# A hybrid decoder layer on one core: other first loads, memory work behind the queries, and another order of the last dense products

## The chip, the core and the metric

The kernel runs on one core of one Trainium2 chip. Every time is in device microseconds (us); a run's time is that of the whole program on that core, and a comparison uses medians of several runs. The profile is one execution with the hardware profiler on. Engines are called as in the profile: PE (TensorE), DVE (VectorE), ACT (ScalarE), POOL (GpSimd), SP (SyncE, which here only issues loads).

## What is computed

One layer for 256 tokens of 1024 channels, with 256 memory tokens. Three branches read the same normalised input: a diagonal state-space layer with a gated unit behind it, a sparse attention (an indexer picks 64 keys for each query), and a cross-attention into the memory. Each is projected up, gated and summed, then projected out; a mixture of 32 experts follows.

```python
h = rms_norm(x, g_mix)
u_ssm, q, k, v, qi, ki, wi, qm, gates = split(h @ w_in)
km, vm = split(rms_norm(mem, g_mem) @ w_mem_kv)
y_ssm = s5_branch(u_ssm, ...)      # ends in y * sigmoid(y @ w_glu)
y_dsa = dsa_branch(q, k, v, qi, ki, wi, positions)
y_mem = memory_branch(qm, km, vm)
g_s, g_d, g_m = split(sigmoid(gates))
merged = g_s * (y_ssm @ w_up_ssm) + g_d * (y_dsa @ w_up_dsa) + g_m * (y_mem @ w_up_mem)
x = x + merged @ w_out
x = x + hier_moe(rms_norm(x, g_ffn), ...)   # 32 experts, 2 chosen for a token
```

## The kernel before

**Dense part.** Every product with a weight of the first part is a `job`, cut into quarters of two 128-row blocks. There are 70 quarters, numbered here 0 to 69 in the order in which the jobs are created: u 0 to 3, a (indexer, keys, values) 4 to 7, q 8 to 11, km, qm and vm (memory keys, queries, values) 12 to 23, the gates 24 to 47, and then the up-projections m 48 to 51 and d 52 to 55, the gated unit glu 56 and 57, the up-projection s 58 to 61, and the output projection o 62 to 69. A quarter's weights (512 KB) are loaded four quarters ahead (`load_quarter`) into the buffers RAW and are split into a high and a low part: ACT copies the high part (L241), DVE subtracts for the low one (L242), into three rotating buffers SPL. `product` then runs twelve matmuls on PE (L257 to L259). In the loop over the quarters, `split(q + 2)` stands ahead of `product(q)`.

**What runs in between.** Three generators, a (attention), s (state space) and m (memory), are advanced one step at a time after each half quarter, as the string table STEPS says. `finish(...)` runs the rest of a generator where its result is needed. The steps use PE for small matmuls, ACT, DVE and POOL. In the attention a `scores` step is PE L739, DVE L815 (mask and maximum), ACT L708 (exponentials), DVE L710 and L712 and POOL L712 (division); a `values` step is PE L718 (transposes), ACT L719, PE L827, then ACT L724 and DVE L725 (`y_split`). The memory's values are PE L883. The state-space layer hands its result to glu through ACT L685 and DVE L686, which write the operand `ysp`; behind glu stand PE L534 (transposes), DVE L693, ACT L695 and DVE L696. `merged_T` transposes the merged branches for the output projection.

**Experts.** 192 pieces of 1 MB of expert weights, two to a matrix, are loaded in order into a ring (RING) of 11 units of two slots each. The slots are those of the dense part; `feed` issues the next piece when its slot is free (`there`), in the dense part by the conditions at the end of the quarter loop, in the expert part when a slot has been read (`release`). A unit that is an entry of GEN2 is one buffer, whose halves come free only together. The experts' products (L1267 gate and up, L1319 down) follow a short router stage.

Instructions go to each engine's queue in an order that a scheduler sets from the program order and priorities; `manual_schedule` keeps program order on the engine named. An engine runs its queue in order.

## Time and profile before

| | |
|---|---|
| time, median of 3 runs | 732.78 us (731.33 to 732.97) |
| time of the profiled execution | 733.47 us |
| its span, first to last instruction | 731.7 us |
| busy in the span: PE, DVE, ACT, POOL | 79%, 42%, 29%, 11% |
| granted PE clock, mean | 0.926 |
| moved by DMA | 246.78 MB |

1.8 us of the profiled execution lie outside its span. The shares are averages over a dense part (to about 280 us) and an expert part with quite different limits, so the rows further down go by stretches.

### The profile page before, as it was taken

To read this page: it belongs to the slowest core of one execution; us is meant where nothing else is said; L and a number is where in the kernel's file an instruction comes from. 1 tells how busy PE (TensorE), PEld (TensorE's weight loads), DVE (VectorE), ACT (ScalarE), POOL (GpSimd) and SP (SyncE) were. 2 spreads that over 40 slices of the span, in tenths; PEclk is the share of its full clock that TensorE was granted. 3 is DMA by queue.
4 is the path that set the end of the run, shared out by engine and by line. 5 is a ranking of instruction groups with operands and counts; after the bars stand their busy time and mean duration, and the time that the engine had idled before them with its cause. 6 is when DMAs were issued, how large, how long until landed. Compare 5 with 4: busy or idle time off the path is not lost.

```text
span 731.7 us, 12785 instructions
## 1 busy us (share of the span) xinstructions
PE 581.6 (79%) x5284; PEld 374.3 (51%) x5284; DVE 308.0 (42%) x772; ACT 211.5 (29%) x426; POOL 77.5 (11%) x122
## 2 busy tenths in 40 slices
PE   8889999999998999888676685495577668469765
PEld 4677787786876786444343252252233324234423
DVE  5999999999574755222120021021111012001102
ACT  6776764648743452111100001000000000000002
POOL 2722201001022001202020020001002002000000
PEclk9999999999999999999996799789879789789989
DMA  8874334436757979999999999999999999999992
GB/s 313 317 217 143 125 118 135 144 118 227 276 175 286 320 299 402 428 425 419 431 424 422 430 428 422 428 427 421 429 426 425 427 426 421 429 426 425 420 409 105
DMA packets 31358, 246.78 MB, mean 337 GB/s; under 512 B 3904, under 2 KB 4544, under 8 KB 15936
## 3 DMA queue, kind: packets, MB, share of 16 engines
q1 hardware_dynamic: 30352, 244.87, 83.4%
q8 instruction: 43, 0.70, 0.4%
q0 software_dynamic: 512, 0.53, 0.3%
q10 hardware_dynamic: 432, 0.52, 0.2%
q14 instruction: 19, 0.16, 0.1%
HBM read 244.33 MB, written 1.05 MB: 335 GB/s over the span
## 4 chain that ended last, share of the span: by engine, by line


## 5 line engine op out<-in xcount | busy, mean ns | idle before, releaser
L1267 PE MATMUL w<-arena 128*32 128x256 f32 x1088 | 125.1, 456 | 43.0 <-DMA arena<-w_up 31.0
L1267 PE MATMUL w<-s,arena 128*32 128x256 f32 x960 | 111.8, 439 | 30.7 <-DMA s<-w_up 29.6
L258 PE MATMUL pj<-s,s 128*128 128x512 f32 (+1 forms) x280 | 112.5, 402 | 4.8 <-DVE s L242 4.8
L257 PE MATMUL pj<-s,s 128*128 128x512 f32 (+1 forms) x280 | 110.0, 405 | 7.0 <-ACT s L241 3.4
L259 PE MATMUL pj<-s,s 128*128 128x512 f32 (+1 forms) x280 | 110.3, 397 | 0.1
L1267 PEld LDWEIGHTS w<-arena 128*32 128x32 f32 x1088 | 55.5, 130 | 90.0 <-DMA arena<-w_up 37.1
L242 DVE TENSOR_TENSOR s<-arena,s 128x1024 fp32r<-128x1024 f32 (+2 forms) x71 | 87.0, 1230 | 21.5 <-ACT s L241 20.9
L241 ACT CAST s<-arena 128x1024 fp32r<-128x1024 f32 (+2 forms) x71 | 72.7, 1029 | 47.3 <-PE pj L259 27.6
L1267 PEld LDWEIGHTS w<-s,arena 128*32 128x32 f32 x960 | 50.5, 125 | 69.0 <-DMA s<-w_up 35.8
L1225 POOL TENSOR_SCALAR s<-early,s 128x32 f32<-128x32 f32 x64 | 32.3, 522 | 350.0 <-PE w L1231 295.6
L1324 DVE COPY arena<-w 32x256 f32<-32x256 f32 x62 | 25.9, 418 | 91.4 <-PE w L1319 78.2
L1324 ACT COPY arena<-w 32x256 f32<-32x256 f32 x62 | 22.5, 364 | 143.7 <-DVE arena L1324 143.7
L257 PEld LDWEIGHTS pj<-s,s 128*128 128x128 f32 x280 | 52.4, 189 | 21.8 <-ACT s L241 6.7
L258 PEld LDWEIGHTS pj<-s,s 128*128 128x128 f32 x280 | 53.1, 190 | 18.8 <-DVE s L242 8.5
L1305 DVE TENSOR_TENSOR early<-w,early 64x256 f32<-64x256 f32 x16 | 6.8, 428 | 126.9 <-ACT early L1304 126.9
L259 PEld LDWEIGHTS pj<-s,s 128*128 128x128 f32 x280 | 53.0, 190 | 10.5 <-DVE s L696 0.5
L1304 ACT ACTIVATE misc<-w 64x256 f32<-64x256 f32 x16 | 6.0, 375 | 137.0 <-PE w L1267 137.0
L1319 PE MATMUL w<-s,s 128*32 128x256 f32 x544 | 34.8, 397 | 10.4 <-DVE s L1310 6.1
L1319 PE MATMUL w<-arena,s 128*32 128x256 f32 x448 | 32.2, 434 | 9.5 <-DMA arena<-w_down 6.0
L1304 ACT ACTIVATE early<-w 64x256 f32<-64x256 f32 x16 | 6.0, 377 | 115.6 <-PE w L1267 115.6
L1305 DVE TENSOR_TENSOR misc<-w,misc 64x256 f32<-64x256 f32 x16 | 6.8, 426 | 72.6 <-ACT misc L1304 72.6
L1260 DVE TENSOR_TENSOR arena<-w,misc 128x256 f32<-128x256 f32 x32 | 12.1, 420 | 57.1 <-PE w L1257 57.1
(307 smaller groups left out, 690.0 us busy)
## 6 DMA issues: line engine op xcount, KB each, us to landing
arena<-w_up SPq DMA_DIRECT2D x15, 2048.0 KB, 29.5
arena<-w_gate SPq DMA_DIRECT2D x13, 2048.0 KB, 29.5
arena<-w_down SPq DMA_DIRECT2D x12, 2048.0 KB, 30.7
s<-w_down SPq DMA_DIRECT2D x12, 2048.0 KB, 31.9
s<-w_gate SPq DMA_DIRECT2D x11, 2048.0 KB, 34.3
s<-w_up SPq DMA_DIRECT2D x9, 2048.0 KB, 34.2
s<-w_up SPq DMA_DIRECT2D x13, 1024.0 KB, 27.1
arena<-w_g SPq DMA_DIRECT2D x24, 512.0 KB, 3.9
```

Of the source, the lines that this page charges most:

```text
L241: S.copy(hi[:, c], src[:, c])
L242: V.tensor_tensor(lo[:, c], src[:, c], hi[:, c], ALU.subtract)
L257: PE.matmul(ps, lhsT=lh, rhs=hi[:, k], start=kt == 0, stop=False)
L258: PE.matmul(ps, lhsT=lh, rhs=lo[:, k], start=False, stop=False)
L259: PE.matmul(ps, lhsT=ll, rhs=hi[:, k], start=False, stop=kt == j["kts"] - 1)
L1225: G.tensor_scalar(dst[:, tt, :], iota[:, 0:CAP], col[:, tt:tt + 1], fac[:, tt:tt + 1], ALU.is_equal, ALU.mult)
L1260: V.tensor_tensor(xe[:, h], xg[:, k:k + 2], b_(gff[:, h], 128), ALU.mult)
L1267: PE.matmul(gu[32 * q:32 * q + 32, :], lhsT=xe[:, kt, 32 * j:32 * j + 32], rhs=w[:, kt % 4, 256 * (q % 2):256 * (q % 2) + 256], start=kt = ...
L1304: S.activation(sg[64:128, :], gu[0:64, :], AF.Silu)
L1305: V.tensor_tensor(hid, gu[64:128, :], sg[64:128, :], ALU.mult)
L1319: PE.matmul(dn[32 * q:32 * q + 32, :], lhsT=hd[:, kb, 32 * c:32 * c + 32], rhs=w[:, kb, 256 * q:256 * q + 256], start=c + kb == 0, stop=c ...
L1324: (S.copy if q % 2 else V.tensor_copy)(Y[32 * j:32 * j + 32, 256 * q:256 * q + 256], dn[32 * q:32 * q + 32, :])
```

## The change

First loads: the first two blocks of the transposed input and g8 are issued from ACT's queue, the weights of quarter 0 from SP's at once; SP keeps program order up to quarter 11 and again from quarter 40. The second half of `x` and `early` are issued behind the first weights of a. The memory tokens are loaded at quarters 8 and 11 rather than 6, qm is computed ahead of km, and the generator m splits its input before it sums its squares.

Last dense products: the order becomes glu (48, 49), m (50 to 53), s (54 to 57), d (58 to 61), then o. `finish(m)` stands at quarter 46, `finish(s)` at 48, `finish(a)` at 58. STEPS spreads the attention's steps out to quarter 60.

Ring: units are taken in another order, by when their slots come free, and `share` paces the pieces during the dense part to 0.75 MB-pieces a quarter with at most two in hand, until the last six quarters.

```diff
-STEPS = ("||s|s|s||sa|a|saa||s|ss|s|s|mm|mm|samm|amm|samm|amm|sa|a|sa|a|sa|a|sa|a|sa|a|sa|a|sam|am|sam|a|sa|a|"
+STEPS = ("|||||s|s|s||sa|a|saa||s|ss|s|sa|sa|sa|a|sam|am|sam|am|samm|am|samm|am|sam|am|sa|a|sam|am|sam|a|sa|a|"
...
-    SP.dma_start(g8, A["g8"])
-    SP.dma_start(xT_raw[:, 0:2], A["xT"][:, 0:2])
+    first = ExitStack()
+    first.enter_context(tc.manual_schedule(engines={mybir.EngineType.SP}))
+
+    S.dma_start(xT_raw[:, 0:2], A["xT"][:, 0:2])
+    S.dma_start(g8, A["g8"])
+    S.dma_start(xT_raw[:, 2:4], A["xT"][:, 2:4])
...
-            for c in ((slice(0, w), slice(w, 2 * w)) if q == 0 else (slice(0, 2 * w),)):
+            for c in ((slice(0, w), slice(w, 2 * w)) if q < 2 else (slice(0, 2 * w),)):
...
-                (V if n == "s" else G).tensor_tensor(m, m, gt, ALU.add)
+                (V if n == "d" else G).tensor_tensor(m, m, gt, ALU.add)
...
-    for n in ('km', 'qm', 'vm'):
+    for n in ('qm', 'km', 'vm'):
...
-    for n in "mdgs":
+    for n in "gmsd":
...
-            new(16, F32R)
-            mgT.extend(sl(s_, 0, 2048, k=8, t=T) for s_ in (16, 6))
+            new(3, F32R)
+            mgT.extend(sl(s_, 0, 2048, k=8, t=T) for s_ in (3, 4))
...
-    RING = ((21, 9), (23, 15), (22, 13), (1, 2), (19, 24), (3, 4), (5, 18), (7, 8), tuple(SPL_[:2]), (16, 6), (SPL_[2], 20))
+    RING = ((21, 9), (1, 2), (23, 13), (5, 18), (22, 15), (16, 6), (19, 24), (7, 8), tuple(SPL_[:2]), (3, 4), (SPL_[2], 20))
...
+            if share[0] < (2 if h is None else 1):
+                return
+            share[0] -= 2 if h is None else 1
...
-        if j is Jkm and i == 0:
+        if j is Jqm and i == 3:
             finish(mmt)
-        if j is Jm[0] and i == 0:
+        if j is Jgd[1] and i == 2:
             finish(mmt)
...
-        if q == 6:
+        if q in (8, 11):
             load_memory()
+        if q == 11:
+            first.close()
...
-        if j is Js[1] and i == 0:
+        if j is Jd[1] and i == 0:
             merged_T(0)
...
+        share[0] = min(share[0] + 0.75, 2) if q < nq - 6 else 1000
...
-        for jj, ss_ in ((Jgd, (1, 2)), (Jd, (24,)), (Js, (3, 4, 5, 18))):
+        for jj, ss_ in ((Jgd, (1, 2)), (Js, (5, 18)), (Jd, (24, 16, 6))):
```

The names of lines below are those of each kernel's own file; the changed file's are a few higher (L242 becomes L247, L686 L689, L725 L728, L815 L818, L739 L742, L718 L721, L827 L830, L883 L886, L708 L711, L710 L713, L712 L715).

DVE's queue, before, from the split of quarter 50 (s_2094) to that of quarter 51; L686 is the low part of `ysp`, L725 the low part of a `y_split` (mm is the memory's, at the attention's).

```order
L242 TENSOR_TENSOR s_2094<-arena,s_2094 128x1024
L706 TENSOR_SCALAR misc<-misc 128x4
L710 RECIPROCAL misc<-misc 128x4
L712 TENSOR_SCALAR arena<-arena,misc 128x256 x3
L725 TENSOR_TENSOR s_1706<-mm,s_1706 128x512
L686 TENSOR_TENSOR s_1999<-arena,s_1999 128x1024
L242 TENSOR_TENSOR s_2112<-arena,s_2112 128x1024
```

The same queue after the change, from the same split of quarter 50 (s_2022) on; the L728 from mm is that of the first half of the memory's values, the L728 from at is the attention's.

```order
L247 TENSOR_TENSOR s_2022<-arena,s_2022 128x1024
L818 ISA arena,misc<-at,arena 128x256
L818 ISA misc 128x1
L818 ISA arena,misc<-at,arena 128x256
L818 ISA misc 128x1
L709 TENSOR_SCALAR misc<-misc 128x4
L713 RECIPROCAL misc<-misc 128x4
L715 TENSOR_SCALAR arena<-arena,misc 128x256 x3
L728 TENSOR_TENSOR s_1436<-mm,s_1436 128x512
L728 TENSOR_TENSOR s_1436<-at,s_1436 128x2x128
```

Behind these stand four more pairs of L818, L728 for the second half of the memory's values, L709 and then L689, the low part of `ysp` (s_1950). Ahead of the split stand two pairs of L818 of the same `scores` step. On ACT the exponentials of that step (four L711), the three L727 that belong to these L728, and then L688, the high part of `ysp`, follow one another. `ysp` is read from quarter 48 on, where before it was read from 56 on; The low part of `ysp` stood five rows behind the split of 50 and now stands twenty behind.

PE's queue after the change, from the last matmuls of the gates (quarter 47) to the first of glu (quarter 48, which reads s_1950, `ysp`).

```order
L742 MATMUL at<-s_76 128x256 x8
L721 MATMUL at<-early,arena 128x128 x4
L721 MATMUL mm<-early,s_77 128x128 x4
L721 MATMUL at<-early,arena 128x128 x4
L830 MATMUL at<-arena,misc 64x128
L886 MATMUL mm<-arena 128x128 x2
L886 MATMUL mm<-s_77,arena 128x128 x2
```

Behind these come four more L886, seven L830, four L742, eight L886 and four L742, and then quarter 48: some fifty small matmuls from the last product of 47 on. Before, matmuls of the same kinds stood four to sixteen at a place between the products of quarters 46 to 54. Counted to the last product of quarter 47, PE's queue held 435 small matmuls before the change and holds 413 after it. The second group of eight L886 uses the one buffer `mm` that L728 reads first.

SP's queue around the router, before; 128x4096 is a piece pair of 2 MB, 128x2048 one piece. Rows of w_o are the last dense loads.

```order
L226 DMA arena<-w_o 128x1024 x2
L983 DMA s_2517<-w_down 128x2048
L983 DMA arena<-w_up 128x4096
L983 DMA s_2542<-w_down 128x2048
L983 DMA s_2558<-w_gate 128x4096
L983 DMA s_2560<-w_up 128x2048
L983 DMA arena<-w_up 128x2048
L1407 TENSOR_LOAD misc
L1407 ISA x2
L983 DMA arena<-w_down 128x2048
L983 DMA arena<-w_gate 128x2048
L983 DMA arena<-w_down 128x2048
```

And after the change.

```order
L231 DMA arena<-w_o 128x1024 x3
L991 DMA s_2426<-w_down 128x4096
L991 DMA arena<-w_gate 128x4096
L991 DMA arena<-w_up 128x4096
L991 DMA s_2522<-w_down 128x2048
L991 DMA s_2547<-w_down 128x2048
L991 DMA s_2563<-w_gate 128x4096
L991 DMA s_2565<-w_up 128x2048
L991 DMA arena<-w_up 128x2048
L1423 TENSOR_LOAD misc
L1423 ISA x2
L991 DMA arena<-w_down 128x2048 x2
```

In both, 22 pieces are issued ahead of the router. Behind it, the second half of w_down now stands ahead of the first half of w_gate, and w_gate goes to a unit of GEN2.

## Rows read from the trace of the kernel before

**Rows 1.** Busy time by stretch: us, engines with instructions, granted clock, DMA share, GB/s.
```profile
core 0: us, PE busy (x) PEld busy (x) DVE busy (x) ACT busy (x) POOL busy (x), PEclk, DMA share, GB/s
...
0.00:20.50 20.50, 16.89 (x62) 10.92 (x63) 11.63 (x35) 12.72 (x22) 3.94 (x11) 1.00 0.86 323
20.50:178.00 157.50, 151.76 (x1124) 119.31 (x1123) 155.91 (x411) 104.64 (x209) 30.41 (x32) 1.00 0.50 163
178.00:196.30 18.30, 17.79 (x107) 14.40 (x106) 10.87 (x24) 12.88 (x19) 0.93 (x1) 1.00 0.79 279
...
207.50:241.60 34.10, 29.07 (x148) 21.91 (x146) 19.08 (x33) 13.72 (x24) 8.97 (x13) 0.95 0.69 251
...
292.20:715.70 423.50, 298.86 (x3376) 154.90 (x3380) 66.84 (x176) 33.85 (x92) 28.66 (x56) 0.88 1.00 424
```

**Rows 2.** Waits of PE, 292 to 715 us: total, times, longest.
```profile
PE w L1267 <- DMA arena<-w_up: 31.0, 10, 4.2
```

**Rows 3.** Timeline of SP's queue around the router: start, us, what is issued.
```profile
292.16 0.33 SPq L983 DMA_DIRECT2D arena<-w_down  x1
292.53 0.43 SPq L983 DMA_DIRECT2D arena<-w_gate  x1
296.59 0.33 SPq L983 DMA_DIRECT2D arena<-w_down  x1
```

**Rows 4.** Waits of DVE, 0 to 20.5 us.
```profile
DVE s L354 <- ACT s L353: 6.1, 2, 5.3
DVE misc L372 <- ACT arena L361: 1.4, 1, 1.4
DVE s L242 <- ACT s L241: 0.9, 1, 0.9
```

**Rows 5.** Timeline of SP's queue at the start.
```profile
1.19 0.41 SPq L194 DMA_DIRECT2D s<-xT  x1
1.66 0.90 SPq L226 DMA_DIRECT2D arena<-w_u  x2
```

**Rows 6.** Groups by line, 178 to 203.8 us (count, busy us, mean ns).
```profile
L242 DVE TENSOR_TENSOR s<-arena,s 128x1024 fp32r<-128x1024 f32 x6 | 7.3, 1222 | 3.3 <-ACT s L241 3.3
...
L712 DVE TENSOR_SCALAR arena<-arena,misc 128x256 f32<-128x256 f32 x6 | 2.4, 457 | 0.0
L719 ACT COPY arena<-at 128x512 f32<-128x512 f32 x4 | 2.2, 581 | 0.0
...
L708 ACT ACTIVATE arena<-arena,misc 128x256 f32<-128x256 f32 x4 | 2.0, 498 | 0.0
...
L815 DVE CUSTOM_DVE_ANT_0 arena<-at,arena 128x256 f32<-128x256 f32 x4 | 1.5, 419 | 2.4 <-PE at L739 2.4
...
L725 DVE TENSOR_TENSOR s<-mm,s 128x512 fp32r<-128x512 f32 x2 | 1.4, 678 | 0.0
...
L685 ACT CAST s<-arena 128x1024 fp32r<-128x1024 f32 x1 | 1.0, 1049 | 0.0
...
L708 ACT ACTIVATION_READ_ACCUMULATOR arena<-arena,misc 128x1 f32 x4 | 0.7, 187 | 0.0
...
L815 DVE DVE_READ_ACCUMULATOR2_ANT misc<- 128x1 f32 x4 | 0.3, 82 | 0.0
```

**Rows 7.** Timeline of PE: a matmul of quarters 48 and 69, first to last.
```profile
194.86 0.40 PE L257 MATMUL pj<-s,s 128*128 128x512 f32 x1
...
276.88 0.62 PE L257 MATMUL pj<-s,s 128*128 128x512 f32 x2
```

**Rows 8.** Timeline of PE: dense matmuls without a break.
```profile
262.78 0.39 PE L257 MATMUL pj<-s,s 128*128 128x512 f32 x1
...
268.45 0.39 PE L259 MATMUL pj<-s,s 128*128 128x512 f32 x1
```

**Rows 9.** Timeline of PE: small matmuls between dense ones.
```profile
212.15 0.64 PE L739 MATMUL at<-s 128*128 128x256 f32 x4
212.62 0.60 PE L718 MATMUL at<-early,arena 128*128 128x128 f32 x4
212.98 0.48 PE L257 MATMUL pj<-s,s 128*128 128x512 f32 x1
```

More of the change, by code (lines that the diff above doesn't have):

```diff
@@ L38 @@
 SLOT = 2048
-STEPS = ("||s|s|s||sa|a|saa||s|ss|s|s|mm|mm|samm|amm|samm|amm|sa|a|sa|a|sa|a|sa|a|sa|a|sa|a|sam|am|sam|a|sa|a|"
-         "sa|a|sam|am|sam|a|sa|a|sa|a|sam|a|sam|a|sam|a|sam|a|sam|a|sam|a|sam|a|sam|a|sam|a|sam|a|sam|a|sam|a|"
-         "sam|a|sam|a|sam|a|sam|a|sam|a|sam|a|sam|a|sam|a|sam|a|sam|a|sa|a|a|a|sa|a|a|a|a||||||||||||s|s|s|s|s"
-         "|s||||||||||||||||||||||").split("|")
+STEPS = ("|||||s|s|s||sa|a|saa||s|ss|s|sa|sa|sa|a|sam|am|sam|am|samm|am|samm|am|sam|am|sa|a|sam|am|sam|a|sa|a|"
+         "sa|a|sam|am|sam|a|sa|a|sa|a|sam|am|sam|m|sam|am|sam|m|sam|am|sam|m|sam|am|sam|m|sam|am|sam|m|sam|am|"
+         "sa||sa|a|sa||sa|a|sa||sa|a|sa||sa|a|sa||sa|a|sa||sa|a|a||sa|a|a||sa|sa|sa|s|sa|sa|a||a|a|a||a|a|a||a"
+         "|a||||||||||||||||||||||").split("|")
 NSLOT = 25
@@ L189, in hybrid_kernel @@
     caus, cneg = sl(24, 0, 512, t=2, s=T), sl(24, 512, 512, t=2, s=T)
-    SP.dma_start(g8, A["g8"])
-    SP.dma_start(xT_raw[:, 0:2], A["xT"][:, 0:2])
+    first = ExitStack()
[3 more added lines that the diff above has]
+    S.dma_start(xT_raw[:, 2:4], A["xT"][:, 2:4])
     warm = sl(24, 0, 512).bitcast(BF16)
     G.memset(warm, 0.0)
-    S.activation(warm[:, 512:513], warm[:, 0:1], AF.Copy, scale=1.0)
+    with tc.high_priority():
+        S.activation(warm[:, 512:513], warm[:, 0:1], AF.Copy, scale=1.0)
     wps = at()
@@ L335, in hybrid_kernel @@
     load_quarter(3)
-    for tt in range(2):
-        SP.dma_start(x_tok[:, tt], A["x"][128 * tt:128 * tt + 128])
+    SP.dma_start(x_tok[:, 0], A["x"][0:128])
     posr, posc = sl(23, 256, 256).bitcast(I32), sl(23, 512, 2).bitcast(I32)
@@ L342, in load_memory @@
     def load_memory():
+        if not mem_there["done"]:
+            SP.dma_start(mT_raw, A["memT"])
+        else:
+            SP.dma_start(mem_tok, A["mem"].rearrange("(t p) d -> p t d", p=128))
         mem_there["done"] = True
-        S.copy(mT_raw[:, 0, 0:1], toks[0][:, 1, 0:1])
-        S.copy(mem_tok[:, 0, 0:1], toks[0][:, 1, 0:1])
-        for dst, src in ((mT_raw, A["memT"]), (mem_tok, A["mem"].rearrange("(t p) d -> p t d", p=128))):
-            SP.dma_start(dst, src)
     def split_T(dst, raw, g):
@@ L382, in hybrid_kernel @@
             split(n_ // 2)
+            if n_ == 1:
+                SP.dma_start(x_tok[:, 1], A["x"][128:256])
     SP.dma_start(early, A["early"])
@@ L844, in memory @@
     def memory():
+        yield from split_T(mT, mT_raw, g8[:, 1])
         sumsq(rm, mem_tok)
@@ L848, in memory @@
         yield
-        yield from split_T(mT, mT_raw, g8[:, 1])
-        for J, tok, dst, g in ((Jkm, toks[0], kmT, "gkm"), (Jqm, toks[2], qmT, "gqm")):
+        for J, tok, dst, g in ((Jqm, toks[2], qmT, "gqm"), (Jkm, toks[0], kmT, "gkm")):
             yield J
@@ L949, in hybrid_kernel @@
     fed = [0]
+    share = [0]
     at_ = {}
@@ L1048, in router_loads @@
         return wr, tri, ones
+    order = ExitStack()
     for q in range(len(quarters)):
         j, i = quarters[q]
-        if j is Jkm and i == 0:
+        if q == 40:
+            order.enter_context(tc.manual_schedule(engines={mybir.EngineType.SP}))
+        if j is Jqm and i == 3:
             finish(mmt)
-        if j is Jm[0] and i == 0:
+        if j is Jgd[1] and i == 2:
             finish(mmt)
@@ L1081, in hybrid_kernel @@
             S.activation(newton[:, 0, 0:1], ssq4[:, 1:2], AF.Sqrt)
-        if mem_normed["done"] and topk_done["done"]:
+        share[0] = min(share[0] + 0.75, 2) if q < nq - 6 else 1000
+        if mem_done["done"] and topk_done["done"]:
             free.add(13)
-        if states_done["done"]:
+        if q >= 43 and states_done["done"]:
             free.update((9, 21))
@@ L1088, in hybrid_kernel @@
             free.add(23)
-        if queried["done"] and not x_back:
+        if q >= 54 and queried["done"] and not x_back:
             SP.dma_start(x_tok, A["x"].rearrange("(t p) d -> p t d", p=128))
             x_back.append(True)
-        if all(g[0] is not att for g in gens):
+        if Jd[0]["done"]:
             if 15 not in free:
@@ L1104, in hybrid_kernel @@
         feed()
-    free.update((16, 6))
+    free.update((3, 4))
     feed()
+    order.close()
     rto = [600]
```

8 lines of the change are left out of this document (3 added, 5 removed).

## The prediction

> **What bounds the kernel now.** I read the windows by stretch first [rows 1]. From 292.2 us on, the DMA share is 1.00 at 424 GB/s: 423.5 us in which the transfers never pause, while PE is busy for 298.86. PE's own largest wait there is for a w_up piece, 31.0 us in all [rows 2]. So the expert part lasts as long as its bytes, and it ends a constant time behind the moment from which the bytes flow without a pause. At 424 GB/s a piece (1.05 million bytes) takes 2.47 us. The reader should see that nothing the change does inside the experts can help, except by starting this stream earlier. The stream starts when the dense part gives its buffers back, so the quantity to forecast is the end of the dense part: the start of quarter 69, 276.88 us [rows 7].
>
> Within the dense part the bound changes. From 20.5 to 178 us DVE is busy 155.91 of 157.5 us, and PE 151.76: both nearly full. From 178 to 196.3 DVE has 10.87 of 18.3, PE 17.79. From 207.5 to 241.6 PE has only 29.07 of 34.10, and a granted clock of 0.95 [rows 1]; that is where PE time is lost late. In the first 20.5 us PE has 16.89, and DVE waits 6.1, 1.4 and 0.9 us [rows 4].
>
> **The change, part by part.**
>
> *First loads.* Both queues feed the first products; the second half of x, `early` and the tables go behind weights. Of DVE's waits, some 5.3 us is the first landing, which stays. What can shrink is the remainder, 0.8 + 1.4 + 0.9 = 3.1 us. But the 1.4 is a wait for ACT's L361, which reads the very x that now lands later; I let it stand. DVE is nearly full until 178 us, so what it gains here reaches quarter 47. I take 1.0 us earlier, with bounds 0 (each weight saved is waited for as x later) and 3.1 (all of it).
>
> The first w_u load is issued 0.47 us behind the first xT load on the one queue [rows 5], and at 323 GB/s the first 20.5 us stay below the 424 seen later [rows 1]. The Trainium skill, page "DMA: Bandwidth & Descriptors", section "Issuing engines are not separate DMA queues", says that DMAs started by different engines run on the same 16 DMA engines and interleave, so a second issuer saves only the time to issue; by that rule the second queue gives about half a microsecond, and what more comes would come from the order. If a second queue did add rate up to 424, the 6.6 MB of the first 20.5 us would need 15.6 us, 4.9 less; the trace of one queue does not decide between them, and my 1.0 is made from DVE's waits alone.
>
> *Up to quarter 48.* Quarter 48 is now glu, and it reads `ysp`. PE's queue holds 413 small matmuls instead of 435 up to the end of quarter 47. Four L739 and four L718 take from 212.15 to 212.98, 0.104 us apiece [rows 9], so PE comes there 22 × 0.104 = 2.3 us earlier, and 1.0 by the front: 194.86 − 3.3 = 191.6. The 2.3 counts in full only if PE and not DVE sets the pace there; DVE's 7.4 us of idle time (18.3 − 10.87) says that it does.
>
> Then comes a chain that nothing covers, because PE is in order and holds only small matmuls (54) between quarters 47 and 48. In DVE's new order: the first scores matmuls, about 0.6 (192.2); two pairs of L818, 2 × (0.42 + 0.08) = 1.0; the split of 50, 1.22 (194.4); two more pairs, 1.0, and the scaling L709, some 0.2 (195.6). ACT's four exponentials with their reads, 4 × (0.50 + 0.19) = 2.75 (198.35). Reciprocal and three divisions, about 0.2 + 3 × 0.457 = 1.55 (199.9). L728, 0.68, which frees `mm` (200.6). Eight L886, 0.83 (201.4). L727, priced by L719's 0.58 (202.0). L688, 1.05: **203.0** [rows 6]. The low part, L689, overlaps with the four products of the high part and six of the next quarter that precede its first reader. So quarter 48 starts 8.1 us later than now. Bounds: 201, if half of the stages overlap with the arriving scores or the front gives its 3.1; 206, if the front gives nothing and a table load or hand-overs add 2.
>
> *From quarter 48 to quarter 69.* Now: 276.88 − 194.86 = 82.0 us. There are 21 × 12 = 252 dense matmuls; 26 of them in a row start from 262.78 to 268.45, 25 gaps, 0.227 each [rows 8], so 57.2 us. With 112 small ones at 0.104, 11.6, that is 68.8, and 13.2 us are excess. Shown of it: 5.0 idle in 207.5 to 241.6 (34.10 − 29.07) and about 1.7 of slow clock (5% of 34.1) [rows 1]. The other 6.5 are short gaps that the modelled ends of matmuls hide.
>
> After the change 32 of the small matmuls have moved ahead of quarter 48, so 57.2 + 80 × 0.104 = 65.5. The excess should shrink, since glu's follow-up (L537, L696, L698, L699) now stands beside products of m, whose operands are ready, and the remaining attention steps are spread over s and d products. I keep 4.8: half of the slow clock, 0.85; 1.0 for `merged_T`, whose transposes in one block now precede the last quarters and whose copy and subtraction stand behind a split; 0.5 for glu's second half; 2.5 of the 6.5. That is 70.3, and quarter 69 starts at 203.0 + 70.3 = **273.3**, 3.6 us earlier. The bounds of the excess are 2 and 11 (all but glu's waits stays).
>
> *Ring and pacing.* In both kernels 22 pieces stand ahead of the router and 14 ahead of the last w_o load. In the first release, two loads were issued at 292.16 and 292.53, and the next at 296.59 [rows 3]; now w_gate goes to a GEN2 unit whose two halves come free together, so only the w_down half follows at once. One piece is 2.47 us, but the queue still holds loads then: I take 0.5 lost, between 0 and 2.5. The pacing changes which pieces land when, not how many by the end of the dense part; I cost it at nothing, covered by the DMA engines' free time (share 0.69 in 207.5 to 241.6 [rows 1]). If that cover were missing, each piece not landed would cost its 2.47.
>
> *Memory.* Loading it at 8 and 11 and computing qm before km moves work, and adds none. It is covered as long as the memory's values are ready at quarter 47, which is the chain above.
>
> **Sum.** −3.6 + 0.5 = −3.1. The profiled execution took 733.47, 0.7 over the median of 732.78, so 730.4 in that execution and a median of **729.7**.
>
> **Rivals.**
>
> *R1, slower: the chain before quarter 48 costs more than the tail returns.* The tail returns 82.0 − 70.3 = 11.7, less 0.5 at the release; it decides against the change from a quarter 48 at 194.86 + 11.2 = 206.1. For it: the chain alternates between four engines, each hand-over adds to it, and the row of 0.95 shows that PE's clock fell after waits. If neither the front nor the 22 matmuls move quarter 47, quarter 48 starts at 206.3, and 2 us of slow clock follow the idle PE: 206.3 + 70.3 + 2 = 278.6, + 0.5, so +2.2: 735.0. Against it: DVE's idle time in 178 to 196.3. Chance 0.19.
>
> *R2, no change: the tail's excess stays.* If the 6.5 us of short gaps are a property of the alternation between kinds of matmul and not of waits, 4 us more remain, and the gain is gone; so it is if one piece fewer has landed at the end of the dense part. 731 to 735. The trace hides these gaps, so I cannot exclude it. Chance 0.23.
>
> *R3, a larger gain: the front.* All 3.1 of DVE's avoidable waits go and the excess falls to 2: 2.1 + 2.8 = 4.9 more, 725. For it: PE lost 3.6 us in the first 20.5 (16.89 busy). Against it: DVE's 1.4 wait depends on x. Chance 0.16.
>
> **How the numbers follow.** The likeliest case has 0.42, and gives 729.7. A measurement tells about 0.3% from no change here, 2.2 us: same is 730.6 to 735.0. The likeliest case lies at its edge, but with R3 the faster side holds 0.58; R2 gives 0.23 to the same, R1 0.19 to slower. The range of 8 in 10 goes from R3's 725, less 1, to R1's 735.0, plus 1 for its clock: 724 to 736. The likeliest case alone goes from 727 (quarter 48 at 201 with 4.8 of excess) to 732.
>
> **What would show it.** In the changed profile: quarter 48 starting at about 203, after PE idles some 6 us behind the last product of 47, waiting for ACT L688; no PE idle time of 5 us in the 34 us behind, and a clock near 1.00 there; quarter 69 at about 273.3; one piece issued at the first release; the DMA share 1.00 some 3 us earlier. DVE's waits in the first 20.5 us should fall by about 1. I am wrong if quarter 48 starts beyond 206, if the time from 48 to 69 is well over 70, or if the full DMA stretch does not move with quarter 69.

## The result, and the profile after

| | before | after |
|---|---|---|
| median (range) | 732.78 (731.33 to 733.43) | 739.66 (735.93 to 739.94) |
| profiled execution, its span | 733.47, 731.7 | 739.66, 737.8 |
| quarter 9 starts | 38.9 | 36.1 |
| quarter 43 starts | 169.7 | 171.6 |
| last product of quarter 47 starts | 194.6 | 198.7 |
| quarter 48 starts | 194.9 | 211.1 |
| quarter 69 starts | 276.9 | 280.8 |

The changed kernel is slower: 1.0088 times the time before, interval 1.0074 to 1.0103 (five runs of each). I had forecast 729.7.

Busy time by stretch of the changed kernel, with the columns of [rows 1]:

```profile
core 0: us, PE busy (x) PEld busy (x) DVE busy (x) ACT busy (x) POOL busy (x), PEclk, DMA share, GB/s
0.00:20.50 20.50, 17.16 (x54) 11.74 (x55) 11.15 (x23) 13.07 (x23) 3.95 (x11) 1.00 0.88 326
20.50:178.00 157.50, 151.46 (x1112) 119.47 (x1110) 153.21 (x398) 97.13 (x184) 25.88 (x30) 0.99 0.49 157
178.00:196.30 18.30, 15.64 (x81) 12.29 (x77) 12.84 (x39) 16.17 (x36) 3.07 (x3) 0.91 0.31 107
198.90:211.10 12.20, 9.89 (x80) 8.15 (x78) 7.24 (x26) 8.22 (x18) 1.23 (x4) 1.00 0.92 357
211.10:245.00 33.90, 33.90 (x174) 27.17 (x176) 22.51 (x29) 17.43 (x27) 4.92 (x4) 1.00 0.61 218
245.00:281.00 36.00, 34.14 (x171) 27.82 (x168) 22.50 (x28) 15.29 (x21) 5.44 (x6) 1.00 0.94 369
296.00:722.00 426.00, 300.21 (x3412) 155.46 (x3404) 66.88 (x176) 33.92 (x92) 29.70 (x59) 0.89 1.00 422
```

Two stretches differ most from [rows 1]. In 178 to 196.3 PE falls from 17.79 us to 15.64 and its clock from 1.00 to 0.91, while ACT rises from 12.88 to 16.17 of 18.3. And behind quarter 48, where PE lost time before (29.07 of 34.10), it is busy for all of 33.90. The expert part is bound as before: share 1.00 at 422 GB/s, only later.

PE's timeline of the changed kernel, from two waits to the first matmul of quarter 69:

```profile
53.66 0.50 PE L262 MATMUL pj<-s,s 128*128 128x512 f32 x1 [1.73 <-ACT s L246]
...
186.69 1.13 PE L262 MATMUL pj<-s,s 128*128 128x512 f32 x2 [2.58 <-ACT s L246]
...
190.18 0.63 PE L263 MATMUL pj<-s,s 128*128 128x512 f32 x1
190.60 0.59 PE L264 MATMUL pj<-s,s 128*128 128x512 f32 x1
191.03 0.39 PE L262 MATMUL pj<-s,s 128*128 128x512 f32 x1
...
198.69 0.39 PE L264 MATMUL pj<-s,s 128*128 128x512 f32 x1
...
207.42 0.71 PE L886 MATMUL mm<-arena 128*128 128x128 f32 x4 [0.74 <-DVE s L728]
...
211.09 0.50 PE L262 MATMUL pj<-s,s 128*128 128x512 f32 x1 [1.15 <-ACT s L688]
...
280.77 0.48 PE L262 MATMUL pj<-s,s 128*128 128x512 f32 x1
```

At 186.69 PE has waited 2.58 us for a cast of ACT, L246. The ten matmuls from 186.69 on then stand 0.43 us apart, up to 191.03, where those of [rows 8] stand 0.227 apart: 2 us more. Why the cast was late is in ACT's own timeline, same kernel (the number in brackets is the wait in front of the instruction; those from 179.97 on stand one behind the other and don't wait; the first two rows are spoken of further down):

```profile
5.66 0.62 ACT L246 CAST s<-arena 128x512 fp32r<-128x512 f32 x1 [2.50 <-DMA arena<-w_u]
...
46.89 1.31 ACT L354 ACTIVATE s<-s,g 128x256 fp32r<-128x256 f32 x3 [2.86 <-DMA s<-memT]
...
179.97 1.28 ACT L685 ACT_TABLE_LOAD   x1
181.27 1.06 ACT L685 ACTIVATE arena<-arena 128x1024 f32<-128x1024 f32 x1
182.34 1.28 ACT L711 ACT_TABLE_LOAD   x1
183.63 0.51 ACT L711 ACTIVATE arena<-arena,misc 128x256 f32<-128x256 f32 x1
...
185.12 0.49 ACT L711 ACTIVATE arena<-arena,misc 128x256 f32<-128x256 f32 x1
...
185.61 1.03 ACT L246 CAST s<-arena 128x1024 fp32r<-128x1024 f32 x1
...
189.46 0.51 ACT L711 ACTIVATE s<-s,misc 128x256 f32<-128x256 f32 x1
```

The same stretch before:

```profile
174.86 0.51 ACT L708 ACTIVATE arena<-arena,misc 128x256 f32<-128x256 f32 x1 [1.37 <-DVE misc L706]
...
177.46 1.28 ACT L682 ACT_TABLE_LOAD   x1
178.75 1.06 ACT L682 ACTIVATE arena<-arena 128x1024 f32<-128x1024 f32 x1
179.72 1.02 ACT L241 CAST s<-arena 128x1024 fp32r<-128x1024 f32 x1
```

Before, the weights' cast follows the gelu at once; four exponentials have gone ahead. After the change a second table load and four exponentials stand between the two, 185.61 − 182.34 = 3.3 us, and the memory's own exponentials follow at 189.46 on top of that. The prediction took nothing from these rows of ACT.

SP's queue around the router, after the change, against [rows 3]:

```profile
290.35 0.33 SPq L991 DMA_DIRECT2D arena<-w_up  x1
297.13 4.76 SPq L991 DMA_DIRECT2D arena<-w_down  x2
301.98 0.86 SPq L991 DMA_DIRECT2D s<-w_gate  x2
```

At the first release only the w_down half goes out at once, its second half some 4.4 us later, and w_gate at 301.98. From 300 to 304 us 1.05 pieces landed where a full stream lands 1.62: 0.57 × 2.47 = 1.4 us.

### The profile page after: what moved, and what is told of

Its sections match the earlier page's. It is cut to its first block, busy times and chain, and to the rows that moved or that the text cites. A ratio compares the mean times of both kernels' runs of the same rounds, so it can differ in the third digit from the quotient of the medians.

```text
span 737.8 us, 12780 instructions
## 1 busy us (share of the span) xinstructions
PE 585.1 (79%) x5284; PEld 378.7 (51%) x5284; DVE 311.2 (42%) x773; ACT 212.3 (29%) x425; POOL 76.9 (10%) x122
## 3 DMA queue, kind: packets, MB, share of 16 engines
HBM read 244.33 MB, written 1.05 MB: 333 GB/s over the span
## 4 chain that ended last, share of the span: by engine, by line
## 5 line engine op out<-in xcount | busy, mean ns | idle before, releaser
L1283 PE MATMUL w<-s,arena 128*32 128x256 f32 x992 | 135.0, 468 | 43.6 <-DMA s<-w_up 37.2
L1283 PE MATMUL w<-arena 128*32 128x256 f32 x1056 | 134.5, 447 | 35.0 <-DMA arena<-w_up 29.2
L1283 PEld LDWEIGHTS w<-s,arena 128*32 128x32 f32 x992 | 58.8, 132 | 87.2 <-DMA s<-w_up 42.7
L247 DVE TENSOR_TENSOR s<-arena,s 128x1024 fp32r<-128x1024 f32 (+2 forms) x72 | 89.8, 1249 | 26.4 <-ACT s L246 26.1
L1283 PEld LDWEIGHTS w<-arena 128*32 128x32 f32 x1056 | 59.4, 128 | 77.6 <-DMA arena<-w_up 33.6
L246 ACT CAST s<-arena 128x1024 fp32r<-128x1024 f32 (+2 forms) x72 | 72.6, 1016 | 50.9 <-PE pj L264 40.4
L262 PEld LDWEIGHTS pj<-s,s 128*128 128x128 f32 x280 | 53.9, 194 | 22.5 <-ACT s L246 5.7
L263 PEld LDWEIGHTS pj<-s,s 128*128 128x128 f32 x280 | 53.9, 193 | 13.6 <-DVE s L247 2.8
L264 PEld LDWEIGHTS pj<-s,s 128*128 128x128 f32 x280 | 54.0, 193 | 12.2 <-DVE s L901 1.5
L1335 PE MATMUL w<-s,s 128*32 128x256 f32 x512 | 32.7, 396 | 9.7 <-DVE s L1326 5.7
```

Source lines behind the costliest of these rows:

```text
L246: S.copy(hi[:, c], src[:, c])
L247: V.tensor_tensor(lo[:, c], src[:, c], hi[:, c], ALU.subtract)
L262: PE.matmul(ps, lhsT=lh, rhs=hi[:, k], start=kt == 0, stop=False)
L263: PE.matmul(ps, lhsT=lh, rhs=lo[:, k], start=False, stop=False)
L264: PE.matmul(ps, lhsT=ll, rhs=hi[:, k], start=False, stop=kt == j["kts"] - 1)
L1283: PE.matmul(gu[32 * q:32 * q + 32, :], lhsT=xe[:, kt, 32 * j:32 * j + 32], rhs=w[:, kt % 4, 256 * (q % 2):256 * (q % 2) + 256], start=kt = ...
```

## Experiments

All times below are of the profiled execution, in us; the median is over all runs of a kernel, and the ratio, with its 95% interval, sets all its runs against runs of the kernel before on the same chip (it is not the quotient of the medians). "end 47" is the start of the last product of quarter 47.

| kernel | median | ratio (95%) | q9 | q43 | end 47 | q48 | q62 | q69 |
|---|---|---|---|---|---|---|---|---|
| before | 732.78 | | 38.9 | 169.7 | 194.6 | 194.9 | 253.9 | 276.9 |
| after | 739.66 | 1.0088 (1.0074–1.0103) | 36.1 | 171.6 | 198.7 | 211.1 | 257.5 | 280.8 |
| no_gelu_table | 735.26 | 1.0055 (1.0034–1.0076) | 34.6 | 168.7 | 191.5 | 204.9 | 251.3 | 274.5 |
| no_pacing | 738.15 | 1.0079 (1.0058–1.0100) | 34.8 | 170.8 | 197.6 | 209.9 | 256.3 | 280.7 |
| ring_swapped | 737.16 | 1.0084 (1.0060–1.0108) | 34.9 | 171.1 | 197.9 | 210.3 | 256.6 | 279.5 |
| memory_earlier | 737.07 | 1.0078 (1.0059–1.0096) | 34.8 | 168.5 | 192.8 | 208.7 | 255.1 | 278.2 |
| attention_later | 744.34 | 1.0167 (1.0149–1.0186) | 34.9 | 172.2 | 199.8 | 210.3 | 263.6 | 287.3 |
| later_swapped_earlier | 744.21 | 1.0161 (1.0147–1.0175) | 34.6 | 168.2 | 192.0 | 208.4 | 261.7 | 285.2 |
| one_queue_start | 738.89 | 1.0094 (1.0080–1.0109) | 35.0 | 171.2 | 198.3 | 210.6 | 257.0 | 280.2 |
| m_first | 737.44 | 1.0066 (1.0051–1.0081) | 35.0 | 172.5 | 199.6 | 207.4 | 256.0 | 281.0 |
| before_glu_first | 732.99 | 1.0025 (1.0011–1.0039) | 38.7 | 169.6 | 194.5 | 202.0 | 253.0 | 276.8 |
| before_m_glu_d_s | 734.43 | 1.0029 (1.0018–1.0040) | 38.5 | 169.1 | 194.1 | 194.3 | 247.2 | 276.5 |
| memory_as_before | 742.49 | 1.0145 (1.0128–1.0162) | 34.7 | 183.7 | 208.8 | 213.8 | 260.2 | 283.3 |
| memory_as_before_swapped | 742.46 | 1.0149 (1.0132–1.0166) | 34.8 | 184.3 | 209.4 | 214.4 | 260.8 | 283.9 |
| glu_first_and_start | 741.27 | 1.0124 (1.0091–1.0157) | 34.9 | 176.7 | 199.6 | 217.7 | 261.0 | 283.7 |
| glu_first_and_memory | 742.67 | 1.0142 (1.0121–1.0164) | 46.0 | 178.4 | 196.5 | 220.2 | 262.4 | 285.2 |
| glu_first_and_steps | 734.91 | 1.0045 (1.0029–1.0061) | 38.6 | 169.4 | 193.2 | 197.7 | 249.5 | 277.1 |

### ACT's queue, the pacing, the ring and the memory's date

*no_gelu_table*: the gelu in the state-space layer becomes a scaled copy, so that no table is loaded for it. The kernel then leaves the gelu out; up to quarter 62 the order on ACT, DVE and POOL is the changed kernel's but for the two loads.

```diff
-S.activation(uT, uT, AF.Gelu_apprx_tanh)
+S.activation(uT, uT, AF.Copy, scale=0.5)
```

> The gelu of the state-space layer (L685) is replaced by a scaled copy, so that ACT's two table loads around it (2 x 1.28 us) fall away; the order of every engine stays. The part of the computation changed is that activation. Theory 'ACT is the bound in quarters 44 to 47' (the cast L246 of a split stands behind table loads, gelu and four exponentials, and PE waits 2.6 us for it and then runs ten matmuls at the lower clock): the wait of L262 on L246 near 184 us goes to about 0, quarter 45 starts near 184 instead of 186.7, the last product of 47 ends near 194.5 instead of 198.9, quarter 69 starts near 276.4 instead of 280.8, and the median falls by about 4 us to some 735. Rival 'the start and the memory wait set the lateness': quarter 69 moves by less than 1 us, since DVE's work takes the time back.

ACT's timeline of this kernel:

```profile
177.07 1.06 ACT L685 ACTIVATE arena<-arena 128x1024 f32<-128x1024 f32 x1
178.04 0.49 ACT L711 ACTIVATE arena<-arena,misc 128x256 f32<-128x256 f32 x1
...
180.00 1.03 ACT L246 CAST s<-arena 128x1024 fp32r<-128x1024 f32 x1
```

From the gelu's place to the cast 2.9 us pass instead of 5.6 from the first table load on. In 178 to 196.3 PE is busy 16.76 us and its clock 1.00 (15.64 and 0.91 with the tables). PE has no wait for L246 left between quarters 43 and 48. Against no_pacing, end 47 comes 6.1 earlier, quarter 48 5.0 and quarter 69 6.2; the medians differ by 2.9. But 2.1 of the 6.1 are there at quarter 43 (168.7 against 170.8) and already at quarter 18 (63.8 against 65.9), more than 100 us ahead of the gelu, and so are not the tables'. Most of them come from PE's clock between 50 and 58 us, first no_gelu_table, then no_pacing (columns as above):

```profile
50.00:58.00 8.00, 6.26 (x28) 4.85 (x29) 7.70 (x16) 7.23 (x13) 0.00 (x0) 1.00 0.73 250
50.00:58.00 8.00, 5.80 (x18) 4.35 (x19) 6.40 (x14) 6.33 (x10) 0.00 (x0) 0.79 0.73 251
```

What the tables cost is read from quarter 43 to end 47: 22.8 us without them, 26.8 in no_pacing, so 4.0. Part of what quarter 69 gains is lost at the release, where the DMA stream loses 0.85 piece, 2.1 us, from 292 to 300 us. How much the kernel before would gain without its tables was not run.

*no_pacing* and *ring_swapped*:

```diff
-share[0] = min(share[0] + 0.75, 2) if q < nq - 6 else 1000
+share[0] = 1000
```

> The changed kernel with share[0] = 1000 after each quarter, so that pieces are issued as soon as their slots are free. Rival 'pacing': with more pieces landed at 270 us (12 to 13 instead of 10.2) the expert stream is ahead by 2 pieces and the time falls by 3 to 5 us to about 735. Theory 'the end of the dense part and the first releases behind it set the time': quarter 69 stays within 1 us of 280.8, the ring's 22 pieces are all there before the second release either way, and the time falls by at most 1.5 us (0.4 of a piece and part of the pause).

```diff
-RING = ((21, 9), (1, 2), (23, 13), ...
+RING = ((21, 9), (23, 13), (1, 2), ...
```

> The changed kernel with the ring's units (23, 13) and (1, 2) exchanged, so that w_gate's halves behind the first release go to single slots again. Theory 'the unit whose halves come free only together costs a pause of the stream at the first release': two half-pieces follow at the first release (about 297 us), the pause between 300 and 305 us (about 0.57 of a piece, 1.4 us) goes, and the time falls by 1.0 to 1.5 us. Rival: the pause is due to the late dense part alone (22 pieces landed before the release), and only moves; time within 0.5 us.

Without pacing, 13.9 pieces have landed by 276 us, against 12.6 in the changed kernel, but none follows until slots come free at 279 (2 GB/s from 276 to 280 us, 414 in the changed kernel). At quarter 69 it is 13.9 against 14.5, and the time hardly moves: the slots set what has landed by then. With the units swapped SP's queue shows a stream again:

```profile
295.85 0.33 SPq L991 DMA_DIRECT2D arena<-w_down  x1
296.27 0.38 SPq L991 DMA_DIRECT2D arena<-w_gate  x1
300.28 0.33 SPq L991 DMA_DIRECT2D arena<-w_down  x1
```

The pause is gone (1.52 pieces from 300 to 304), so the unit of two halves makes it in the changed kernel. Its 1.4 us is not shown by the ratios: 1.0084 for this kernel, 1.0079 for no_pacing on the same chip, with intervals wider than 1.4 us. Nor is no_pacing a yardstick for it: with the unit of two halves it has no pause there either (420 GB/s from 300 to 304 us), since its stream stood still earlier, from 276 to 280, and the loads issued ahead of the release were still under way (the last landed at 303.0 us, at 300.8 in the changed kernel).

*memory_earlier* and *attention_later*:

```diff
-if q in (8, 11):
+if q in (5, 8):
```

> The changed kernel with the memory tokens loaded at quarters 5 and 8 instead of 8 and 11. Theory 'ACT waits for the memory tokens': its wait of 2.9 us at 44 to 47 us goes, PE's waits in quarter 14 (2.2 us, then nine matmuls at the lower clock) go, and quarter 15 starts near 54 instead of 57.4. If the gain lasts, quarter 43 starts 2 to 3 us earlier than 171.6 and the time falls by about 2.5 us; rival 'DVE is full from 60 to 178 us and nothing lasts': quarter 43 within 0.7 us of 171.6, time unchanged. The order of ACT near the gelu changes too (the gelu stands later, behind one more cast), so quarters 44 to 48 are read apart.

In attention_later the steps `a` of STEPS in quarters 39 to 47 move to 48 to 57; the rows of those quarters become:

```diff
-"sa||sa|a|sa||sa|a|sa||sa|a|sa||sa|a|sa||sa|a|sa||sa|a|a||sa|a|a||sa|sa|sa|s|sa|sa|a||a|a|a||a|a|a||a"
+"sa||sa|a|sa||sa|a|s||s||s||s||s||s||s||s||||sa|a|a|a|sa|sa|sa|sa|sa|sa|a|a|a|a|a|a|a|a|a|a|a|a|||||||"
```

> The changed kernel with the attention's steps of quarters 39 to 47 moved behind quarter 48 in STEPS. The order then holds 21 small matmuls between the last product of 47 and quarter 48 instead of 54, and the scores step with its four exponentials, reciprocal and divisions is gone from there. Theory 'the late ysp comes from attention work that stands ahead of the memory's values and of L688': the stretch from the last product of 47 (198.7) to quarter 48 (211.1), 12.4 us, falls to about 7, and quarter 48 starts near 205. Some of it is given back behind 58, where 32 small matmuls now stand at quarters 59 and 60 (1 to 2 us): quarter 69 near 277, time down by 3 to 4 us, about 736. Rival 'the memory's softmax is late by itself': quarter 48 stays above 209 and the time within 1 us.

later_swapped_earlier has the edits of attention_later, ring_swapped and memory_earlier together.

> Three edits together: attention's steps moved behind 48, units (23, 13) and (1, 2) of the ring exchanged, memory tokens loaded at 5 and 8. If their causes are separate, their gains add: 3.5 + 1.2 + 1.2 = about 6 us, a median of 733 to 734, level with the kernel before. If the end of the dense part moves to 275 but the ring's 22 pieces are all landed before the first release, a pause of up to 2 us stays and the median is about 735.

Loading the memory three quarters earlier shortens ACT's wait for the tokens from 3.4 us (no_pacing) to 0.5, and the clock from 50 to 58 us is 1.00. Quarter 43 comes 2.3 earlier than in no_pacing and end 47 4.8, but quarter 48 by only 1.2: the stretch between the last two grows from 12.3 to 15.9. (The order on ACT and DVE is another in this kernel, with the gelu behind one more cast, so the 2.5 us between quarter 43 and end 47 have more than one cause.) PE's timeline of memory_earlier shows what holds it:

```profile
192.81 0.39 PE L264 MATMUL pj<-s,s 128*128 128x512 f32 x1
...
195.22 0.50 PE L742 MATMUL at<-s 128*128 128x256 f32 x2 [1.58 <-DVE s L736]
197.20 0.97 PE L742 MATMUL at<-s 128*128 128x256 f32 x6 [1.48 <-DVE s L736]
```

The attention's scores L742 wait 3.1 us for L736, the low part of the attention's queries; behind them the chain takes 11.5 us (197.20 to 208.67), as it does in the changed kernel (12.0, from 199.06). So a PE that arrives earlier meets a side chain on ACT and DVE that is not ready. Taking attention out of that stretch shortens it to 10.5, not by its full PE time, and quarter 48 comes no earlier (210.3): the memory's own steps stay, as PE's timeline of attention_later shows:

```profile
206.66 0.71 PE L886 MATMUL mm<-arena 128*128 128x128 f32 x4 [1.40 <-DVE s L728]
...
210.33 0.50 PE L262 MATMUL pj<-s,s 128*128 128x512 f32 x1 [1.62 <-ACT s L688]
```

and the attention's steps, moved into the up-projections, come due at quarters 58 to 60, which then take 18.2 us (242.3 to 260.5) instead of 9.4. Against no_pacing it loses 6.6 at quarter 69. The three together keep the earlier end 47 (192.0), need 16.4 us from there to quarter 48, and lose the rest in the up-projections, as attention_later does: the gains do not add.

### Two queues at the start, and which product goes first

*one_queue_start*: all first loads on SP's queue, as before.

```diff
-    S.dma_start(xT_raw[:, 0:2], A["xT"][:, 0:2])
-    S.dma_start(g8, A["g8"])
-    S.dma_start(xT_raw[:, 2:4], A["xT"][:, 2:4])
+    SP.dma_start(g8, A["g8"])
+    SP.dma_start(xT_raw[:, 0:2], A["xT"][:, 0:2])
...
+    load_quarter(0)
+    SP.dma_start(xT_raw[:, 2:4], A["xT"][:, 2:4])
```

> The changed kernel with the first loads again on SP's queue alone, g8 and xT ahead of the weights of quarter 0. Theory 'the second queue shares the same transfer rate and only changes which load lands first': quarter 0 starts near 6.2 instead of 7.4, ACT's wait of 2.5 us for w_u goes, quarter 4 starts within 0.7 us of before, and the end moves by less than 1 us. Rival 'two queues bring 1 us or more': quarter 4 and the end come 1 us or more later than with two queues.

Quarter 0 starts at 6.2 instead of 7.36, and quarter 9 at 35.0, as with two queues in the other runs (34.6 to 35.0). The second queue is worth nothing; the rest of the new opening, the order of the loads above all, gives the 3 to 4 us at quarter 9. The profiled execution of the changed kernel lost some of that (36.1): the twelve matmuls of quarter 0 stand 0.43 apart, from 7.36 to 12.65 us, and its quarter 4 starts at 21.3, where the other runs with this opening have 19.7 to 20.1.

*m_first*: m ahead of glu.

```diff
-for n in "gmsd":
+for n in "mgsd":
```

> The changed kernel with the up-projection m ahead of glu (mgsd instead of gmsd), so that quarter 48 reads the first half of the memory's values and ysp is read from quarter 52. Theory 'the chain up to ysp holds PE': eight L886 and L688 (0.8 + 1.05 us) and the wait of 1.1 us leave the chain; quarter 48 starts near 208, quarter 69 2 to 3 us earlier, time about 737. Rival 'the memory's values are what is late': quarter 48 starts earlier but quarter 49 or 50 waits for the second half, and quarter 69 moves by less than 1 us.

Quarter 48 starts 3.7 earlier, at 207.4, and the gain is gone by quarter 56 (238.8): with glu behind m, glu's own result is waited for: the transposes behind it, PE's L537 at 231.01, wait 1.20 us for its L302 on ACT. Quarter 69 moves by 0.2, as the rival had it.

### The order alone, on the kernel before

*before_glu_first*: glu first on the kernel before, with its s steps of quarters 56 to 58 at 48 to 50. The order is gmds, d still ahead of s, where the change has gmsd.

```diff
-for n in "mdgs":
+for n in "gmds":
```

> The kernel before with one part of the change alone: glu ahead of m (gmds instead of mdgs) and its steps in STEPS moved from quarter 56 to 48; first loads, memory, attention's steps, ring and pacing as before. Theory 'glu first exposes the chain memory values, ysp, glu, whatever the rest does': the last product of 47 ends at 194.6 as before, quarter 48 starts near 202 instead of 194.9, the stretch from 48 to 69 gets some 5 us shorter, and quarter 69 and the time move by +1 to +3 us (734 to 735). Rival 'the order is a gain and only the late quarters 43 to 47 spoil it': quarter 48 starts before 199 and the time falls by 2 us or more.

*before_m_glu_d_s*: likewise, with glu behind m and the s steps at 52 to 54.

```diff
-for n in "mdgs":
+for n in "mgds":
```

> The kernel before with the order m, glu, d, s (mgds): m covers the memory's values and ysp, d covers glu's own result, and the attention gets two more quarters. Quarter 48 starts at 194.9 as before, glu at about 211 without a wait, the gaps of 1.5 us at quarter 56 and 1.2 us at 57 go, and those of the attention at 52 and 54 (2.0 and 2.0) shrink: quarter 69 near 273 instead of 276.9 and the time about 729, 3 us under before. Rival 'the excess of the tail is not waits': quarter 69 within 1 us of 276.9, time unchanged.

PE's timeline of before_glu_first:

```profile
194.53 0.39 PE L259 MATMUL pj<-s,s 128*128 128x512 f32 x1
...
201.96 0.50 PE L257 MATMUL pj<-s,s 128*128 128x512 f32 x1 [3.36 <-ACT s L685]
```

Glu first costs 7.1 us at quarter 48, and all of it is back by quarter 69 (276.8 against 276.9). Glu first alone costs at most 0.4% (1.0025, 1.0011 to 1.0039). With glu behind m nothing is lost at 48, and quarter 62 starts 6.7 earlier, but between 64 and 69 that goes too. The loss is in quarters 65 and 66 (13.1 us instead of 5.8), as PE's timeline of before_m_glu_d_s shows:

```profile
262.09 1.08 PE L1035 MATMUL mm<-s,arena 128*128 128x36 f32 x8 [0.68 <-ACT arena L1021]
...
264.54 0.75 PE L257 MATMUL pj<-s,s 128*128 128x512 f32 x2 [0.47 <-ACT s L241]
```

The router's small matmuls (L1035) stand ahead of quarter 66 there, the cast that quarter 66 waits for stands behind a table load on ACT (262.06), and from 264.5 to 270.2 us the granted clock is 0.55. Late weights show there only as 0.20 us of ACT's next cast (264.69).

### Which part of the change makes the order cost

*memory_as_before*: the changed kernel with the memory's loads, their order and the head of the generator m as before; memory_as_before_swapped has ring_swapped's edit as well.

```diff
-    for n in ('qm', 'km', 'vm'):
+    for n in ('km', 'qm', 'vm'):
...
-        if j is Jqm and i == 3:
+        if j is Jkm and i == 0:
...
-        if q in (8, 11):
+        if q == 6:
```

> The changed kernel with the memory's part as it was: tokens loaded together at quarter 6, km ahead of qm, the squares summed ahead of the split of the input. STEPS, the order gmsd, ring and pacing stay as changed. In its order the memory's second softmax stands ahead of the gelu on ACT, the exp table is loaded again only behind L688, and 12 small matmuls stand between the last product of 47 and quarter 48 instead of 54. Theory 'the memory that comes behind the queries runs into the gelu and the attention at quarters 44 to 48': the last product of 47 ends near 194 instead of 198.7, quarter 48 starts near 199 instead of 211.1, quarter 69 near 269 instead of 280.8, and the time falls by 4 to 8 us to 731 to 735 (less than the 11 us, since the pieces are paced and the ring holds 22). Rival 'DVE's total work up to ysp is what is late': quarter 48 stays above 207 and the time falls by less than 2 us.

> The same with the ring's units (23, 13) and (1, 2) exchanged. With the dense part early the ring's 22 pieces land before the second release, so that the pause behind the first release is longer (about 2 us) and its removal is worth more: 1.5 to 2.5 us under the run above, 729 to 733. Rival: the pause only moves, within 0.5 us of the run above.

The stretch from end 47 to quarter 48 falls to 5.0, as it should if the memory's chain gates it; quarters 43 to 48 take 30.1 instead of 39.5. But attention's steps moved ahead as well (20 rows of small matmuls in that stretch instead of 78), so this is not the memory alone. And the kernel is slower, and the swapped ring changes nothing in that (742.46 against 742.49), since quarters 15 to 18 take 25 us instead of 9.4 (11.4 in the kernel before). There PE's trace has 148 rows of small matmuls, against 12 in the changed kernel; DVE is busy 23.77 of 25 us in 57 to 82, with the state-space layer's and the attention's preparation, and PE waits for it (longest 2.6). Why the scheduler puts these steps there is open.

The last three are before_glu_first with one part of the change each: glu_first_and_start the first loads and SP's order, glu_first_and_memory the memory's loads and order with STEPS of quarters 6 to 23, glu_first_and_steps the STEPS of quarters 24 to 47. What each adds, in its first lines:

```diff
+    S.dma_start(xT_raw[:, 0:2], A["xT"][:, 0:2])
...
+        if q in (8, 11):
...
+          "a||sa|a|sa||sa|a|a||sas|as|as|as|as|s||||||||||||||||||||||||||||||||||||||").split("|")
```

> The kernel before with glu first (quarter 48 at 202.0 and about 733.0 us) and, added, the new first loads alone: two queues, second half of x and early behind weights, SP in program order up to quarter 11. Theory 'the start is not the cause': quarter 9 comes 2 to 4 us earlier, quarter 43 within 1.5 us of 169.6, quarter 48 within 1.5 us of 202, time 732 to 734. Rival 'PE's earlier start lets the dense part run ahead of the memory': quarter 48 beyond 205 and 2 us or more slower.

> The kernel before with glu first and, added, the memory's part alone: tokens loaded at quarters 8 and 11, qm ahead of km, the input split ahead of the squares, the changed STEPS in quarters 6 to 23. Theory 'memory behind the queries brings its second softmax to the gelu': the last product of 47 ends beyond 197, quarter 48 starts beyond 207, time 736 to 739. Rival: quarter 48 within 2 us of 202, time within 1.5 us of 733.

> The kernel before with glu first and, added, the changed STEPS of quarters 24 to 47 alone (the attention's steps spread out, the memory's steps two to a quarter up to 34). Theory 'memory, not attention': the memory's softmax comes earlier, quarter 48 at 202 or before it, time 731 to 734. Rival 'attention's spread steps crowd ACT and DVE before quarter 48': quarter 48 beyond 205, time 2 us or more slower.

Beside glu first alone (quarter 48 at 202.0) the new steps bring quarter 48 to 197.7, and lose that again by quarter 69. Each of the other two pushes quarter 48 out, to 217.7 and 220.2, further than the whole change does (211.1). But glu_first_and_memory does not test later loads. SP's queue at its start:

```profile
13.41 0.33 SPq L344 DMA_DIRECT2D s<-memT  x1
...
16.02 0.38 SPq L346 DMA_DIRECT2D s<-mem  x1
```

Without SP's program order up to quarter 11, which belongs to the part with the first loads, the memory tokens are issued at 13.41 and 16.02 us, among the first weights; the kernel before issues them at 24.55 and 25.03, the changed one at 38.03 and 47.41. Quarter 9 of this kernel starts at 46.0. What later loads alone do was not run.

The first loads with SP's order did what their edit says: quarter 9 comes 3.8 us earlier than in before_glu_first, and quarter 69 6.9 later. So the parts don't add: with glu first, this one alone puts the state-space result later than the whole change does. Its loss begins where memory_as_before has its own, in quarters 15 to 18 (20.4 us, 83 rows of small matmuls).

## Why the prediction was wrong, step by step

**The step that failed: the arrival at the end of quarter 47, forecast 191.6, measured 198.7.** It rested on two terms: 1.0 from the front and 22 fewer small matmuls, 2.3, which "counts in full only if PE and not DVE sets the pace there". Both failed. By quarter 43 the front's gain is gone, 1.9 later instead of 1.0 earlier: 2.9 of the 7.1. From quarter 43 to end 47, where fewer matmuls should have saved time, 27.1 us pass instead of 24.9. There neither PE nor DVE set the pace; ACT did, with 16.17 of 18.3 us busy. I had looked for the next limit at DVE's idle time and had not walked ACT's queue, where the gelu's table loads, attention's exponentials and the memory's softmax now follow one another ahead of a cast that the next quarter needs. PE's wait of 2.58 and the 2 us at the lower clock behind it make 4.6 of this stretch; without the tables it takes 22.8, 4.0 less than in no_pacing. Loading the memory three quarters earlier gives 4.8 at end 47, 2.3 of it by quarter 43. The two were not run together, so whether their gains add is open.

**First loads, forecast 1.0 earlier.** Quarter 9 came 2.8 earlier, more than forecast. Quarter 15 came at 57.4 as before (57.3), since ACT's L354 waits 2.86 us for the memory tokens, until 46.89, and PE then 1.73 for the cast behind it, at 53.66, with a clock of 0.79 from 50 to 58 us (1.00 before). Quarter 18 is 1.9 earlier once more, quarter 30 3.6 later, quarter 43 1.9 later. That "DVE is nearly full until 178 us, so what it gains here reaches quarter 47" was wrong: from 20.5 to 178 us DVE's idle time rose from 1.59 to 4.29 us. The memory's date has a large part in this, as memory_earlier has quarter 30 3.5 earlier than no_pacing and quarter 43 2.3; which steps lose the time between quarters 18 and 30 is open.

**From end 47 to quarter 48, forecast 11.4, measured 12.4.** The mechanism is right: 211.09 − 198.69, the links of the chain follow as forecast, and the waits stand where they were put (L728's `mm`, then L688). The 1.0 more is in the eight L886 behind L728, priced at 0.83: they are sixteen rows of the trace and take 1.8 us, from 207.42 until L742 follows at 209.23. That the term fits so well is in part luck, since PE came late. The prediction let the chain begin with PE's arrival. Where PE arrives as forecast, the scores wait for the attention's queries: 0.8 us in no_gelu_table (arrival 191.5, stretch 13.4), 3.1 in memory_earlier (192.8, 15.9). Quarter 48 then starts at 204.9 and 208.7, not at 203.0, and no_gelu_table, with the forecast arrival, still takes 734.06 us in its profiled execution.

**From quarter 48 to 69, forecast 70.3, measured 69.7.** Right: the excess shrank, no idle time of PE in the 34 us behind 48 and a clock of 1.00. Its parts are less sure than the sum: the prediction counted 112 and 80 small matmuls, the trace has 144 and 88 rows of them, so that at the same 0.104 the excess before is 9.8 instead of 13.2, and 3.3 is left after the change instead of 4.8. The up-projections behind glu do what was forecast, but m_first and before_m_glu_d_s show that such a gain can be lost again by quarter 56 or behind 64.

**The release, forecast 0.5, measured 1.4**: the term was mis-sized, the mechanism right (ring_swapped). **Pieces landed by quarter 69, forecast no change, measured 0.4 fewer** (14.5 against 14.9): 1.0 us.

**The sum:** 7.1 + 1.0 − 0.6 + 0.9 + 1.0 = 9.4, and 739.66 − 9.4 = 730.3, where the forecast for the profiled execution was 730.4. The third term is the tail's, 69.7 − 70.3.

**The rivals.** R1, slower, named the right place and the right rule: the change loses from a quarter 48 at 206.1, and it came at 211.1. It also asked what happens if neither the front nor the 22 matmuls move quarter 47, and they did not. But its price for that was 206.3, with quarter 47 as before, and its mechanism a longer chain; the chain took 1.0 more, and the lateness came in ahead of it. R2 (the tail's excess stays) and R3 (a larger gain at the front) are refuted for this kernel.

**Shown and argued.** Shown: that ACT's queue delays the cast, and that the tables are worth 4.0 us there (the rows of after, no_gelu_table); that glu first alone costs at most 0.4% (before_glu_first); that an earlier arrival of PE need not reach quarter 48 (1.2 of 4.8 us do in memory_earlier, 5.0 of 6.1 in no_gelu_table); and the pause at the release (ring_swapped). Only argued: that the memory's date takes the front's gain away by quarter 43, since moving it reorders ACT and DVE as well; and that the start hurts in glu_first_and_start because the dense part runs ahead of the small steps. The 1.4 us of the pause stay a count of pieces, since the ratios don't show them. Open: why the scheduler puts the memory's softmax behind the gelu once the memory is later, and which version would keep both the front's 3 us and the tail's; no combination that was run beats the kernel before.

## What to carry to other kernels

When a result becomes due earlier, walk every engine's in-order queue through the stretch before the new date, not only the engine that was full there: the one that feeds the casts (here ACT, with table loads in the middle) can become the limit, though DVE had seven idle microseconds there in the profile before. A dense part that starts earlier or runs ahead can lose it all again where a side chain of small steps gates the next product (in memory_earlier 4.8 us at end 47 became 1.2 at quarter 48). Parts that are tried one by one don't add: here the first loads alone, with glu first, cost more than the whole change. And look in the trace at what an edit did: one of the runs meant to load the memory later loaded it earlier.
